# A float32 hybrid decoder trunk: three 256-column products per contraction step become one of 512 and one of 256, in another column order and at other addresses

## Chip, cores and metric

One core of one Trainium2 chip. The metric is the device time of one launch in microseconds (us). Before the change the median of three runs is 1567.65 us (1567.45 to 1567.79).

## What is computed

One decoder layer on 256 tokens with 16 learned meta tokens put ahead of them, model width 2048, all in float32. Cut to what matters:

```python
def rmsnorm(x, g):
    return x * lax.rsqrt(jnp.mean(x * x, axis=-1, keepdims=True) + EPS) * g
...
proj = xn @ w_in                  # 2048 -> 13336 columns: q, k, v, gates of both branches
o_fox = forgetting_attention(fq, fk, fv, ff, b_forget)      # 8 heads of 128
o_gla = gated_linear_attention(gq, gk, gv, g_log)           # 4 heads, chunks of 64
y = sigmoid(gate_fox) * (o_fox @ w_o_fox) + sigmoid(gate_gla) * (o_gla @ w_o_gla)
h = h + y @ w_out
h = h + square(relu(rmsnorm(h) @ w_ff1)) @ w_ff2            # 2048 -> 8192 -> 2048
return rmsnorm(h)[:, N_META:]
```

## The kernel before, in words

Activations are held transposed: channels on the 128 partitions, tokens along the row. A **row tile** is 128 output channels for all tokens; its contraction over 2048 channels runs in 16 steps of 128, here called **k-steps**. Float32 precision is had by splitting: each operand is a high part (rounded to the fp32r format) and a low part (the remainder), and a k-step is three fp32r products that accumulate in one PSUM bank: high weights by high activations, high weights by low activations, low weights by high activations (lines 153, 154 and 155, in `gemm`). Each product has its own load of 128x128 weights into the array. A **token tile** has 256 columns. A **meta tile**, for keys and values, has 272 (the 256 tokens and then the 16 meta tokens).

`stream()` is the order of the row tiles: linear attention (GLA) per head, forgetting attention (FoX) per head, then per output tile two pairs of gates, half a tile each of `of` (FoX outputs) and a tile of `og` (GLA outputs), then 16 tiles on `y` (the output projection), then four rounds of 16 tiles on `x2` (ff1) and 16 on `a` (ff2). Seven tiles of the first stage run side by side while the input arrives (lines 345, 346 and 348). For each tile SyncE loads two halves of the weights (512 KB each), ScalarE rounds them to the high part (`whi`, line 133) and VectorE subtracts for the low part (`wlo`, line 134). Five buffers of each are used in turn, so a half is prepared when TensorE is done with the half five before it. The schedule of each engine is made when the program is built, from this order.

Row tiles alternate between three PSUM banks (pool `pg`). A finished tile is read out of its bank by VectorE in one operation: into `evt` with the norm's factor for gates (lines 464 and 811), into the residual `h` (line 852, `add_residual`), into `evt` with the maximum and the factor for ff1 (line 871, `relu2`), then squared (line 873) and split again into `a` (lines 168 and 169). `in_order` (lines 164 and 165) puts a meta tile's 16 columns back ahead of the tokens in two operations.

Addresses are chosen already: `operand` lays `y`, `of`, `og`, `x2` and `a` out with the high and low parts of 128 tokens in turn, `at` words from the start of the buffer, and `kick` puts the last k-step of `y` and `of` 32 words further (class `Rows`).

Of the kernel before, what the change touches and what calls it, by code (L numbers as in the profile page):

```python
# [7 lines left out]
F32 = mybir.dt.float32  # L8
# [29 lines left out]


class Rows:  # L40

    def __init__(self, most, last):
        self.most, self.last, self.n = most, last, most.shape[1]
        self.shape = [most.shape[0], self.n + 1, *most.shape[2:]]

    def __getitem__(self, at):
        p, k, *rest = at
        if k < self.n:
            return self.most[(p, k, *rest)]
        return self.last[(p, 0, *rest)]  # L50
# [28 lines left out]
def trunk(ctx: ExitStack, tc: tile.TileContext, hT, w_small, w_all, consts, w_alpha2, out):  # L79
# [68 lines left out]
    def gemm(w, x, k0=0, nk=KT, pool=None):  # L148

        ps = bank(pool or pg, "ps")[:, 0 : x.shape[3] if len(x.shape) == 4 else NT]  # L150
        for k in range(nk):
            hi, lo = w(k0 + k)
            nc.tensor.matmul(ps, hi, x[:, k, 0], start=(k == 0), stop=False)  # L153
            nc.tensor.matmul(ps, hi, x[:, k, 1], start=False, stop=False)  # L154
            nc.tensor.matmul(ps, lo, x[:, k, 0], start=False, stop=(k == nk - 1))  # L155
        issued()
        return ps

    def eviction():
        return tmp.tile([P, NT], F32, tag="evt", name=nm("evt"), bufs=2)  # L160

    def in_order(dst, ps, r):

        nc.vector.tensor_tensor(dst[:, NM:NA], ps[:, 0:NT], r[:, NM:NA], op=ALU.mult)
        nc.vector.tensor_tensor(dst[:, 0:NM], ps[:, NT:NA], r[:, 0:NM], op=ALU.mult)
# [45 lines left out]
    def operand(pool, name, nk=KT, at=0, kick=0, **kw):  # L211

        t = pool.tile([P, at + nk * 2 * NT + kick], F32R, name=nm(name), **kw)

        def rows(k, n, at):
            return t[:, at + k * 2 * NT : at + (k + n) * 2 * NT].rearrange("p (k a o t) -> p k o a t", a=2, o=2, t=P)

        return Rows(rows(0, nk - 1, at), rows(nk - 1, 1, at + kick)) if kick else rows(0, nk, at)

    def pair(ap):  # L220
        return ap.rearrange("p (a t) -> p a t", t=P)
# [4 lines left out]
    ROW = 5 * P  # L226
    x_row = keep.tile([P, 64 + KT * ROW], F32R, tag="s1", name="x")[:, 64:]
    xa = x_row.rearrange("p (k o t) -> p k o t", o=2, t=ROW // 2)[:, :, :, 0:NA]
    x_hi, x_lo, x = xa[:, :, 0, :], xa[:, :, 1, :], xa[:, :, :, 0:NT]

    cons = const.tile([P, 425], F32, name="cons")
# [3 lines left out]
    room = keep.tile([P, KT * 2 * NT], F32, tag="s2", name="room")  # L235
# [28 lines left out]
    def first_weights(c0, n, k0):  # L264
        raw = wp.tile([P, HK * P], F32, tag="raw", name=nm("raw"), bufs=RAW)
        hi = wp.tile([P, HK, P], F32R, tag="whi", name=nm("whi"))
        lo = wp.tile([P, HK, P], F32R, tag="wlo", name=nm("wlo"))
# [18 lines left out]
    def square(q):  # L286
        sq = acc if q == 0 else sqs[q % 2]
        nc.scalar.activation(sq, h[:, 4 * q : 4 * q + 4, 0:NA], AF.Square)
        if q:
            nc.vector.tensor_tensor(acc, acc, sq, op=ALU.add)  # L290

# [21 lines left out]
    for s in range(KT // 2):  # L313
# [5 lines left out]
        for kk in range(2):  # L319
            k = 2 * s + kk  # L320
            nc.scalar.activation(x_hi[:, k, 0:NT], h[:, k, NM:NA], AF.Identity, scale=gain(0, k))
            nc.vector.scalar_tensor_tensor(x_lo[:, k, 0:NT], h[:, k, NM:NA], gain(0, k),
                                           x_hi[:, k, 0:NT].bitcast(F32), op0=ALU.mult, op1=ALU.subtract)
            xm = meta[:, k, :]
            nc.gpsimd.tensor_tensor(xm, h[:, k, 0:NM], gain(0, k).to_broadcast([P, NM]), op=ALU.mult)
            nc.gpsimd.tensor_copy(x_hi[:, k, NT:NA], xm)
            nc.gpsimd.tensor_tensor(x_lo[:, k, NT:NA], xm, x_hi[:, k, NT:NA].bitcast(F32), op=ALU.subtract)
# [11 lines left out]
        def products(c, k, part):  # L339
            hi, lo = at[c][0][:, k % 2, :], at[c][1][:, k % 2, :]  # L340
            ps, st, sp = first_ps[c], k == 0, k == KT - 1
            xs = (x if c < NF - 1 else xa)[:, k]
            ps = ps[:, 0 : xs.shape[2]]
            if part == 0:
                nc.tensor.matmul(ps, hi, xs[:, 0], start=st, stop=False)  # L345
                nc.tensor.matmul(ps, hi, xs[:, 1], start=False, stop=False)  # L346
            else:
                nc.tensor.matmul(ps, lo, xs[:, 0], start=False, stop=sp)  # L348
# [110 lines left out]
    def gla_gates(ts):  # L459
        sg = att.tile([P, 4, NT], F32, tag="sg", name=nm("sg"))  # L460
        for i in range(4):
            src = gemm(next_weights(), x) if ts is None else ts[:, i, :]
            t = eviction()
            nc.vector.tensor_tensor(t, src, rbt, op=ALU.mult)
# [26 lines left out]
    def gla_head(hd, sg, ready=None):  # L491
# [11 lines left out]
        def keys(i, ps):  # L503
# [3 lines left out]
            for g, q, n, c in ((0, 0, NM, NT), (0, NM, C - NM, 0), (0, 2 * C, C, C - NM), (1, 0, C, 2 * C - NM),  # L507
                               (1, 2 * C, C, 3 * C - NM)):
                p = (c + NM) % NA
                nc.vector.tensor_tensor(kx[:, i, g, q : q + n], ps[:, c : c + n], en[:, i, p : p + n], op=ALU.mult)  # L510
            nc.vector.tensor_tensor(kz[:, i], *(ap.unsqueeze(1).to_broadcast([P, 4, NB])
                                                for ap in (ps[:, NT - NB : NT], en[:, i, 4 * C :])), op=ALU.mult)

        if ready:
            ps = gemm(next_weights(), xa)
            keys(0, ready[1])
            keys(1, ps)
        else:
            for i in range(2):
                keys(i, gemm(next_weights(), xa))  # L520
        for i in range(2):
            t = ready[0][:, i, :] if ready else gemm(next_weights(), x)
# [62 lines left out]
        for i in range(4):  # L585
            ps = gemm(next_weights(), xa)
            vT = tmp.tile([P, NA], F32, tag="vT", name=nm("vT"))
            in_order(vT, ps, rb)
# [463 lines left out]
```

## Time and profile before

| what | value |
|---|---|
| median of three runs | 1567.65 us |
| the profiled execution | 1567.48 us; its span 1565.8 us, so 1.7 us lie around the span |
| granted TensorE clock, mean | 0.998 |
| TensorE busy with products / with weight loads | 1556.1 / 1553.6 us, 13460 of each |
| VectorE / ScalarE / GpSimd busy | 990.9 / 730.3 / 110.0 us |
| read from memory | 289.32 MB, 187 GB/s on the mean |

How to read it: "PE" rows are products, "PEld" rows are weight loads, and the two run beside each other. A product's recorded duration includes the way through the array, so 276 ns of one does not mean that the next starts 276 ns later; the pace is read from start to start, or from a stretch of time divided by the products in it. "DVE" is VectorE, "ACT" ScalarE, "POOL" GpSimd. An "x770" in a stretch counts products that touch it.

### The profile page before, as it was taken

The numbers are of one execution on the slowest core, as the hardware profiler recorded it, in microseconds if no ns is written. First come the engines' busy times: TensorE is split into PE (matmuls) and PEld (weight loads), VectorE is DVE, ScalarE is ACT, GpSimd is POOL, SyncE is SP. The second block draws the span as 40 slices with busy tenths as digits, with TensorE's granted clock in tenths as the row PEclk, the third lists the DMA queues.
The fourth block names the chain that finished last, engine by engine and source line by source line (L and its number), as shares of the span: only waits on it lengthen the run. The fifth ranks groups of instructions, "written<-read, shape, count | busy, mean of one in ns | idle before, by whom it ended". The sixth has DMA issues, their size and how long they took to land.

```text
span 1565.8 us, 32259 instructions
## 1 busy us (share of the span) xinstructions
PE 1556.1 (99%) x13460; PEld 1553.6 (99%) x13460; DVE 990.9 (63%) x1485; ACT 730.3 (47%) x1006; POOL 110.0 (7%) x197
## 2 busy tenths in 40 slices
PE   9999999999999999999999999999999999999997
PEld 9999999999999999999999999999999999999997
DVE  7897757576665555555666765556655665566655
ACT  6665343444444444444555443344433444344553
POOL 7012000021100000000011000000000000000022
PEclk9999999999999999999999999999999999999999
DMA  9544545555555655656555556566565565665552
GB/s 327 175 150 157 185 157 181 164 194 169 165 162 179 197 190 196 195 191 194 195 192 195 192 191 198 191 196 194 192 197 193 195 195 192 197 192 193 196 183 103
DMA packets 86626, 293.53 MB, mean 187 GB/s; under 512 B 9112, under 2 KB 16800, under 8 KB 86352
## 3 DMA queue, kind: packets, MB, share of 16 engines
q1 hardware_dynamic: 85872, 289.62, 56.8%
q8 instruction: 106, 1.74, 0.4%
q0 software_dynamic: 176, 1.12, 0.2%
q10 hardware_dynamic: 432, 0.72, 0.1%
q14 instruction: 40, 0.33, 0.1%
HBM read 289.32 MB, written 2.11 MB: 186 GB/s over the span
## 4 chain that ended last, share of the span: by engine, by line
PE 99%; POOL 0%; issue 0%; DVE 0%; POOLq 0%; ACT 0%; ACTq 0%
PE ps L154 31%; PE ps L153 31%; PE ps L155 31%; PE ps L345 1%; PE ps L346 1%; PE ps L348 1%; PE ps L921 1%; PE pa L547 1%; PE ps L905 0%; PE po L610 0%; PE warm L308 0%; POOL o L969 0%; PE po L181 0%; PE psa L652 0%; PE pq L726 0%
## 5 line engine op out<-in xcount | busy, mean ns | idle before, releaser
L133 ACT CAST whi<-raw 128x1024 fp32r<-128x1024 f32 x522 | 549.3, 1053 | 752.1 <-PE ps L154 681.5
L134 DVE TENSOR_TENSOR wlo<-raw,whi 128x1024 fp32r<-128x1024 f32 x522 | 639.6, 1226 | 398.0 <-ACT whi L133 388.0
L153 PE MATMUL ps<-x,whi 128*128 128x256 f32 (+1 forms) x2576 | 723.0, 281 | 0.0
L154 PE MATMUL ps<-x,whi 128*128 128x256 f32 (+1 forms) x2576 | 719.6, 279 | 0.0
L155 PE MATMUL ps<-x,wlo 128*128 128x256 f32 (+1 forms) x2576 | 719.5, 279 | 0.0
L155 PEld LDWEIGHTS ps<-x,wlo 128*128 128x128 f32 x2576 | 484.8, 188 | 0.0
L154 PEld LDWEIGHTS ps<-x,whi 128*128 128x128 f32 x2576 | 484.5, 188 | 0.0
L153 PEld LDWEIGHTS ps<-x,whi 128*128 128x128 f32 x2576 | 484.3, 188 | 0.0
L153 PE MATMUL ps<-a,whi 128*128 128x256 f32 x960 | 265.0, 276 | 0.0
L154 PE MATMUL ps<-a,whi 128*128 128x256 f32 x960 | 265.0, 276 | 0.0
L155 PE MATMUL ps<-a,wlo 128*128 128x256 f32 x960 | 265.0, 276 | 0.0
L153 PEld LDWEIGHTS ps<-a,whi 128*128 128x128 f32 x960 | 180.2, 188 | 0.0
L154 PEld LDWEIGHTS ps<-a,whi 128*128 128x128 f32 x960 | 180.2, 188 | 0.0
L155 PEld LDWEIGHTS ps<-a,wlo 128*128 128x128 f32 x960 | 180.2, 188 | 0.0
L849 POOL TENSOR_TENSOR acc<-acc,hsq 128x256 f32<-128x256 f32 x26 | 29.1, 1118 | 747.1 <-ACT hsq L848 747.1
L154 PE MATMUL ps<-y,whi 128*128 128x256 f32 x256 | 70.8, 276 | 0.0
L153 PE MATMUL ps<-y,whi 128*128 128x256 f32 x256 | 70.7, 276 | 0.0
L155 PE MATMUL ps<-y,wlo 128*128 128x256 f32 x256 | 70.7, 276 | 0.0
L154 PE MATMUL ps<-og,whi 128*128 128x256 f32 x256 | 70.7, 276 | 0.0
L153 PE MATMUL ps<-og,whi 128*128 128x256 f32 x256 | 70.7, 276 | 0.0
L155 PE MATMUL ps<-og,wlo 128*128 128x256 f32 x256 | 70.7, 276 | 0.0
L852 DVE TENSOR_TENSOR h<-ps,h 128x256 f32<-128x256 f32 x76 | 32.3, 425 | 39.6 <-PE ps L155 39.6
(296 smaller groups left out, 1455.1 us busy)
## 6 DMA issues: line engine op xcount, KB each, us to landing
raw<-w_all_dram SPq DMA_DIRECT2D x537, 512.0 KB, 4.0
raw<-w_all_dram SPq DMA_DIRECT2D x8, 384.0 KB, 6.6
h<-hT_dram SPq DMA_DIRECT2D x8, 275.0 KB, 6.9
negc<-fdram POOLq DMA_DIRECT2D x1, 1088.0 KB, 7.6
out_dram<-o SPq DMA_DIRECT2D x2, 512.0 KB, 2.6
raw<-w_all_dram SPq DMA_DIRECT2D x2, 256.0 KB, 3.6
room<-w_small_dram SPq DMA_DIRECT2D x1, 320.0 KB, 7.5
out_dram<-o ACTq DMA_DIRECT2D x1, 320.0 KB, 3.1
```

What stands on the lines that cost most here:

```text
L133: nc.scalar.copy(hi[:, k, :], r)
L134: nc.vector.tensor_tensor(lo[:, k, :], r, hi[:, k, :].bitcast(F32), op=ALU.subtract)
L153: nc.tensor.matmul(ps, hi, x[:, k, 0], start=(k == 0), stop=False)
L154: nc.tensor.matmul(ps, hi, x[:, k, 1], start=False, stop=False)
L155: nc.tensor.matmul(ps, lo, x[:, k, 0], start=False, stop=(k == nk - 1))
L345: nc.tensor.matmul(ps, hi, xs[:, 0], start=st, stop=False)
L346: nc.tensor.matmul(ps, hi, xs[:, 1], start=False, stop=False)
L348: nc.tensor.matmul(ps, lo, xs[:, 0], start=False, stop=sp)
L547: nc.tensor.matmul(dst, k[:, a], q[:, a, :], start=(a == 0), stop=(a == 1))
L849: nc.gpsimd.tensor_tensor(acc, acc, sq, op=ALU.add)
L852: nc.vector.tensor_tensor(ht[:, j, :], ps, ht[:, j, :], op=ALU.add)
L921: nc.tensor.matmul(ps[:, NT:], w(k)[0], a[:, k, :, t0 // P], start=(k == 0), stop=(k == KT - 1))
```

## The change

1. **Token tiles.** A k-step is now two products (`mac2`, lines 143 and 144). The high weights take the high and low parts of the activations side by side, 512 columns, into a whole bank; the low weights take the 256 high columns, into its first half. The bank's two halves are added when the tile is read out (`total`): ScalarE copies the second half to SBUF, VectorE adds it to the first. For the residual, `add_residual` has a copy and two additions.
2. **Meta tiles** keep three products of 272 (`mac3`, lines 148, 150 and 152). The row of x is now meta, tokens (high), tokens (low), meta (low), so the low product lands 16 columns further, and `join` adds its 16 meta columns back (a ScalarE copy and a VectorE addition of 16 columns). Columns come out in their own order: `in_order` goes, and `keys` has two operations in place of six.
3. **Order of the columns.** Every such product reads its activations and writes its bank through `steps`: four words, then the four that lie 16 words on, and so on through the row, in four passes.
4. **Addresses.** A 16-word tile `gap` between the pools moves every `wlo` by 64 bytes; x, `y`, `of` and `a` start at other offsets (`a` at 0, 4, 48 and 0 words in the four rounds); `kick` and `Rows` go.
5. **Small ones.** The gates' multiplication goes from VectorE to GpSimd; the corners of a FoX group are split in one pair of operations in place of four; six of the first seven tiles are read by a copy and an addition in place of a copy.

The core of the diff:

```diff
-    def gemm(w, x, k0=0, nk=KT, pool=None):
-        ps = bank(pool or pg, "ps")[:, 0 : x.shape[3] if len(x.shape) == 4 else NT]
+    def steps(ap):
+        return ap.rearrange("p (i a e) -> p a i e", a=4, e=4)
+    def mac2(ps, hi, lo, x, first, last):
+        nc.tensor.matmul(steps(ps), hi, steps(row(x)), start=first, stop=False)
+        nc.tensor.matmul(steps(ps[:, 0:NT]), lo, steps(x[:, 0, :]), start=False, stop=last)
+    def mac3(ps, hi, lo, k, first, last):
+        if hi is not None:
+            nc.tensor.matmul(steps(ps[:, X_LO]), hi, steps(x_lo[:, k]), start=first, stop=False, skip_group_check=True)
+        if lo is not None:
+            nc.tensor.matmul(steps(ps[:, 0:NA]), lo, steps(x_hi[:, k]), start=False, stop=last and hi is None, skip_group_check=True)
+        if hi is not None:
+            nc.tensor.matmul(steps(ps[:, 0:NA]), hi, steps(x_hi[:, k]), start=False, stop=last, skip_group_check=True)
+    def gemm2(w, x, k0=0, nk=KT, pool=None):
+        ps = bank(pool or pg, "ps")
         for k in range(nk):
             hi, lo = w(k0 + k)
-            nc.tensor.matmul(ps, hi, x[:, k, 0], start=(k == 0), stop=False)
-            nc.tensor.matmul(ps, hi, x[:, k, 1], start=False, stop=False)
-            nc.tensor.matmul(ps, lo, x[:, k, 0], start=False, stop=(k == nk - 1))
+            mac2(ps, hi, lo, x[:, k], k == 0, k == nk - 1)
...
+    def join(ps):
+        b = tmp.tile([P, NM], F32, tag="join", name=nm("join"))
+        nc.scalar.copy(b, ps[:, NA : NA + NM])
+        nc.vector.tensor_tensor(ps[:, 0:NM], ps[:, 0:NM], b, op=ALU.add)
+    def total(ps, t=None):
+        b = tmp.tile([P, NT], F32, tag="evb", name=nm("evb"))
+        nc.scalar.copy(b, ps[:, NT:512])
...
+        nc.vector.tensor_tensor(t, ps[:, 0:NT], b, op=ALU.add)
+        return t
...
     def relu2(a, f, ps):
-        t = eviction()
-        nc.vector.scalar_tensor_tensor(t, ps, 0.0, r2b, op0=ALU.max, op1=ALU.mult)
+        t = total(ps)
+        nc.vector.scalar_tensor_tensor(t, t, 0.0, r2b, op0=ALU.max, op1=ALU.mult)
```

TensorE's queue in FoX, where a meta tile ends and a token tile begins. Before (the two rows between are transposes of a finished tile):

```order
L153 MATMUL ps_4271<-x,whi_4266 128x272
L154 MATMUL ps_4271<-x,whi_4266 128x272
L155 MATMUL ps_4271<-x,wlo_4267 128x272
L759 MATMUL pv_4320<-cons,vT_4247 128x128
L760 MATMUL pv_4320<-cons,vT_4247 128x128
L153 MATMUL ps_4342<-x,whi_4331 128x256
L154 MATMUL ps_4342<-x,whi_4331 128x256
L155 MATMUL ps_4342<-x,wlo_4332 128x256
```

Now, at the end of a meta tile of GLA and the start of the token tile behind it; the last numbers are the counts of the column order, four passes of 17, 32 or 16 runs of four:

```order
L148 MATMUL psa_2967<-x,whi_2962 128x4x17x4
L150 MATMUL psa_2967<-x,wlo_2963 128x4x17x4
L152 MATMUL psa_2967<-x,whi_2962 128x4x17x4
L143 MATMUL ps_3033<-x,whi_3022 128x4x32x4
L144 MATMUL ps_3033<-x,wlo_3023 128x4x16x4
```

A meta tile's k-step has three products as it had, in the order high, low, high weights; a token tile's has two, each a single instruction. In the whole program the products fall from 13372 to 9724.

VectorE's queue in ff1, from one reading out of a bank to the next, before:

```order
L871 SCALAR_TENSOR_TENSOR evt_13497<-ps_13448,r2b 128x256
L873 TENSOR_TENSOR asq_13499<-evt_13497 128x256
L134 TENSOR_TENSOR wlo_13639<-raw_13637,whi_13638 128x1024
L169 TENSOR_TENSOR a_12899<-asq_13499,a_12899 128x2x128
L134 TENSOR_TENSOR wlo_13645<-raw_13643,whi_13644 128x1024
```

and now:

```order
L184 TENSOR_TENSOR evt_11633<-ps_11598,evb_11631 128x256
L892 SCALAR_TENSOR_TENSOR evt_11633<-evt_11633,r2b 128x256
L894 TENSOR_TENSOR asq_11636<-evt_11633 128x256
L121 TENSOR_TENSOR wlo_11756<-raw_11754,whi_11755 128x1024
L189 TENSOR_TENSOR a_11207<-asq_11636,a_11207 128x256
L121 TENSOR_TENSOR wlo_11804<-raw_11802,whi_11803 128x1024
```

One operation of 256 columns is added ahead of the others. It waits for ScalarE's copy `evb`, which stands between two weight roundings in ScalarE's queue:

```order
L120 CAST whi_11749<-raw_11748 128x1024
L181 COPY evb_11631<-ps_11598 128x256
L120 CAST whi_11755<-raw_11754 128x1024
L188 CAST a_11207<-asq_11636 128x256
L120 CAST whi_11803<-raw_11802 128x1024
```

The copy is the new row; the rounding of `a` stood between the weight roundings before too. The loads and their order are the same 564 in SyncE's queue.

More of the change, by code (lines that the diff above doesn't have):

```diff
@@ L290, in square, with gap @@
             nc.vector.tensor_tensor(acc, acc, sq, op=ALU.add)
+    def gap():
+        if "gap" not in stages:
+            stages["gap"] = wp.tile([P, 16], F32, tag="gap", name="gap", bufs=1)
     stages = {}
@@ L341, in products @@
             ps, st, sp = first_ps[c], k == 0, k == KT - 1
[L342 to L346, printed above, removed]
+            if c == NF - 1:
+                mac3(ps, hi if part == 0 else None, lo if part else None, k, st, sp and part == 1)
+            elif part == 0:
+                nc.tensor.matmul(steps(ps), hi, steps(row(x[:, k])), start=st, stop=False)
             else:
[L348 removed]
+                nc.tensor.matmul(steps(ps[:, 0:NT]), lo, steps(x[:, k, 0]), start=False, stop=sp)
         if s < KT // 2 - 1:
```

163 lines of the change are left out of this document (81 added, 82 removed).

## The prediction

> **What bounds the kernel now.** I read the page's totals and chain first, then TensorE's waits, then stretches of TensorE's time by stage, then single products and loads.
>
> ```profile
> span 1565.8 us, 32259 instructions
> PE 1556.1 (99%) x13460; PEld 1553.6 (99%) x13460; DVE 990.9 (63%) x1485; ACT 730.3 (47%) x1006; POOL 110.0 (7%) x197
> PE 99%; POOL 0%; issue 0%; DVE 0%; POOLq 0%; ACT 0%; ACTq 0%
> PE warm L308 <- DVE ones L188: 1.3, 1, 1.3
> PE pn L945 <- ACT sq L926: 0.7, 1, 0.7
> ```
>
> TensorE is the bound from end to end: 99% of the chain is its own, and it waits twice, for 2.0 us together. Time can only come from a shorter product pace. The stretches give it (start, end and length in us, products that touch it, granted clock, DMA share, GB/s):
>
> ```profile
> 946.30:1033.34 87.04, 87.04 (x770) 1.00 0.60 194
> 172.70:184.01 11.31, 11.31 (x98) 1.00 0.62 206
> 49.28:67.04 17.76, 17.76 (x147) 1.00 0.60 196
> 0.00:49.28 49.28, 47.97 (x379) 1.00 0.87 287
> ```
>
> The first is a round of ff2, 16 tiles of 16 k-steps: 87.04 / 256 = 0.3400 us per k-step, 113.3 ns per product of 256 columns. The second is two token tiles of GLA: 11.31 / 32 = 353.4 ns, 117.8 per product, for the same instructions at the same clock. So at least 4.5 ns of a product are not columns: they depend on how the streams fall together. The third is three meta tiles: 17.76 / 48 = 370.0 ns, 123.3 per product of 272. The fourth, the first seven tiles, runs with the DMA engines 87% busy.
>
> Is a product paced by its columns or by its weights? The weight loads (mean ns last before the idle time):
>
> ```profile
> L153 PEld LDWEIGHTS ps<-a,whi 128*128 128x128 f32 x960 | 180.2, 188 | 0.0
> L547 PEld LDWEIGHTS pa<-qx,kx 128*128 128x128 f32 x32 | 4.9, 190 | 0.1
> L547 PEld LDWEIGHTS pa<-qx,kx 128*64 128x64 f32 x32 | 2.2, 137 | 0.7
> ```
>
> A load of 128 columns lasts 53 ns longer than one of 64, so 128 stream in about 106 ns. That is 94% of the 113.3 ns: loads and columns go side by side, both without a gap, and 7.3 ns of each product are hand-over or collision.
>
> **The change, part by part.** The count comes from the groups kept apart by shape:
>
> ```profile
> L153 PE MATMUL ps<-x,whi 128*128 128x256 f32 x1952 | 542.1, 278 | 0.0
> L154 PE MATMUL ps<-x,whi 128*128 128x256 f32 x1952 | 540.5, 277 | 0.0
> L155 PE MATMUL ps<-x,wlo 128*128 128x256 f32 x1952 | 540.4, 277 | 0.0
> L153 PE MATMUL ps<-a,whi 128*128 128x256 f32 x960 | 265.0, 276 | 0.0
> L153 PE MATMUL ps<-x,whi 128*128 128x272 f32 x624 | 180.9, 290 | 0.0
> L153 PE MATMUL ps<-y,whi 128*128 128x256 f32 x256 | 70.7, 276 | 0.0
> L153 PE MATMUL ps<-og,whi 128*128 128x256 f32 x256 | 70.7, 276 | 0.0
> L153 PE MATMUL ps<-of,whi 128*128 128x256 f32 x128 | 35.4, 278 | 0.0
> ```
>
> Token k-steps: 1952 + 960 + 256 + 256 + 128 = 3552. (A further 96 in the first stage and 640 of 272.)
>
> *The pair of 512 and 256.* No 512-column product stands in the trace, so it is bounded. While a 512 runs, the load for the 256 behind it has twice its time and is done early; while the 256 runs, the next load again has only that long, so I leave the 256 at 113.3. Low end: the 512 streams at the load's pace with nothing added, 2 x 106 = 212, and the k-step is 212 + 113.3 = 325.3. High end, from the nearest product whose columns outlast its load, the 272: 123.3 less 106 x 272/256 = 112.6 leaves 10.7, so 212 + 10.7 + 113.3 = 336.0. If columns cost what they cost now, 768 x 113.3/256 = 340.0, and nothing is gained; if every product falls into the slow pace, 353.4. I take **328.5**, a third of the way up between the first two: in a 272 the load streams through 94% of the product, in a 512 through half, so less of the 10.7 should be met. Saved per k-step 11.5 ns, x 3552 = **-40.8 us** (ends -52.2 and -14.2; with the others 0 and +47.6).
>
> The Trainium skill, "TensorE: Matmul & The Clock Gate", section "Back-to-back issue gap", gives N/2.4 + 2.5 ns for a warm product alone, an estimate of 215.8 + 109.2 = 325.0 per k-step here and 53 us saved. Its 109.2 for 256 columns is 4.1 below the 113.3 measured, so the measurement decides for the 256.
>
> *The slow pace.* The token group of x and x2 lasts 542.1 us where 1952 of `a`'s 276 ns would be 538.8; with its two sisters (540.5 and 540.4) the excess is at most 6.6 us, and part of it lies at changes to other work. New addresses may end it or spread it: **-2 us** (0 to -6.6).
>
> *Meta tiles.* 640 k-steps keep three products and three loads. Columns and addresses change, the count doesn't: **0**, between -15 (three of 112.6 + 3 in place of 370) and +9 (13.4 each, the step between the two paces).
>
> *First stage.* Its 96 token k-steps could give 96 x 11.5 = 1.1 us, but the row above has DMA near its limit there: **0**.
>
> *Reading out.* Each of the 3552 / 16 = 222 token tiles gains a ScalarE copy and a VectorE addition:
>
> ```profile
> L134 DVE TENSOR_TENSOR wlo<-raw,whi 128x1024 fp32r<-128x1024 f32 x522 | 639.6, 1226 | 398.0 <-ACT whi L133 388.0
> L852 DVE TENSOR_TENSOR h<-ps,h 128x256 f32<-128x256 f32 x76 | 32.3, 425 | 39.6 <-PE ps L155 39.6
> L133 ACT CAST whi<-raw 128x1024 fp32r<-128x1024 f32 x522 | 549.3, 1053 | 752.1 <-PE ps L154 681.5 <-issue 60.9 <-ACT hsq L848 1.9
> L168 ACT CAST a<-asq 128x256 fp32r<-128x256 f32 x64 | 25.9, 406 | 0.1
> 80.00:90.00 10.00, 10.00 (x86) 9.62 (x84) 10.00 (x31) 5.12 (x9) 1.35 (x2) 1.00 0.32 106
> ```
>
> The program has 174 more VectorE additions and 265 more ScalarE copies, small ones among them; at 425 and 406 ns that is at most 74 and 108 us, or 70% and 55% of a span of 1524. TensorE's products hide it: ScalarE's idle 752 us ahead of the roundings is for TensorE (681.5) to give up buffers, so preparation runs ahead. The narrow place is GLA's first heads, where VectorE is busy for all 10 us of a stretch (third pair in the row); there the tiles are mostly meta tiles, whose six or two operations become fewer. If this cover went, each late addition would show with its 0.43 us.
>
> *Hand-overs between stages.* An ff1 round's last tile feeds ff2's 16th k-step:
>
> ```profile
> 1120.51 1.05 ACT L133 CAST whi<-raw 128x1024 fp32r<-128x1024 f32 x1 [1.67 <-PE ps L154]
> 1120.58 0.43 DVE L871 SCALAR_TENSOR_TENSOR evt<-ps,r2b 128x256 f32<-128x256 f32 x1 [0.48 <-PE ps L155]
> 1121.50 0.41 ACT L168 CAST a<-asq 128x256 fp32r<-128x256 f32 x1
> 1122.74 0.42 DVE L169 TENSOR_TENSOR a<-asq,a 128x256 fp32r<-128x256 f32 x1
> ```
>
> ff2 began at 1120.38 and wants the last `a` 15 k-steps later, at 1125.5; it is ready at 1123.16, 2.3 us early. Now the copy stands behind the rounding that starts as the tile ends: 1120.51 + 1.05 + 0.41 + 0.43 = 1122.40 for the maximum that began at 1120.58, so 1.8 us later, or 3.0 if a `wlo` of 1.23 slips between. The wanted time comes 15 x 11.5 ns = 0.2 us sooner, so 2.1 us of slack are left: 0 to 0.9 us of waiting at each of four such places and one ahead of x2: **+1 us** (0 to +4).
>
> *Sum*, on the profiled execution: 1565.8 - 40.8 - 2 + 0 + 0 + 1 = 1524.0, and 1.7 around the span: **1525.7 us**, against 1567.48 for that execution, which is 0.2 below the median.
>
> **The rivals.**
>
> *More is gained.* If the steps keep reads of weights and of columns apart, the k-step goes to 325.3 and the meta tiles lose 15: 1565.8 - 52.2 - 2 - 15 + 1 + 1.7 = **1499**. For it: 4.5 ns per product already come and go with the pace alone. Against: nothing of the steps' effect is in the trace.
>
> *Less is gained.* Columns, not loads, pace the product. For it: 113.3/256 and 123.3/272 are 0.443 and 0.453 ns per column, nearly one rate. At 336.0: **1552**; at 340.0, with the slow pace gone, **1566**, no change. Against: 117.8 for the same 256 columns. That the change isn't carried out is ruled out by the queues: each 512 is one instruction.
>
> *Slower: the runs of four collide more.* Every product jumps 16 words after each four, on the way in and in the bank. If that throws each load and column stream into the slow pace, a k-step is 353.4: +47.6, less some 4 already paid: 1565.8 + 43.6 + 1 + 1.7 = **1612**. It decides from a 512 product of over 226.7 ns beside a 256 of 113.3. For it: the paces of 113.3 and 117.8 show that the way two streams fall together matters, and one of them now changes place every four words. Against: each run is read and written whole, four words on end.
>
> The Trainium skill, "Advanced Engine Details and Errata", section "PSUM Cachelines", says that a bank's pattern with gaps slows products significantly, and in the next line that two neighbours on end are what best throughput needs. By its first line this rival comes; by its second, runs of four are free. No product of the trace writes with gaps, so no run here shows which.
>
> **How the numbers follow.** Forecast, k-step 325 to 333: 1511 to 1541, chance 0.50. More gained, 1488 to 1511: 0.14. Less, 1541 to 1564: 0.13. Within 0.2% (3.1 us, about what a measurement of this kernel can tell from no change): 0.05. Slower, around 1612: 0.18. So faster 0.77, same 0.05, slower 0.18. The range goes from the more-gained case's end through no change with its width, 1488 to 1572, and leaves out the slower rival.
>
> **What would show it.** ff2's rounds: 84.1 us for 256 k-steps in place of 87.04. Starts 215 ns apart behind a 512 and 113 behind a 256 confirm the hand-over; 227 and 113 say that columns pace; 109 behind a 256 says that the load wasn't the limit. Meta tiles away from 370 ns per k-step say that order and addresses act by themselves. VectorE or ScalarE as what TensorE waits for, by more than the 2.0 us of before, would make the reading-out wrong. A k-step over 340 makes the whole forecast wrong.

## The result, and the profile after

The changed kernel takes **1567.36 us** (median of 12 runs, 1566.89 to 1567.79), the kernel before 1567.84 us on the same chip (12 runs, 1567.45 to 1568.13): a ratio of 0.9997, 95% interval 0.9988 to 1.0006. The change makes no difference that can be measured. The profiled execution took 1566.89 us, its span 1565.1.

The page of the changed kernel:

```profile
span 1565.1 us, 25427 instructions
PE 1553.5 (99%) x9812; PEld 1408.5 (90%) x9812; DVE 1060.0 (68%) x1659; ACT 790.4 (50%) x1271; POOL 128.2 (8%) x213
PE 97%; ACT 1%; DVE 1%; issue 0%; DMA 0%; POOL 0%; SPq 0%; POOLq 0%; ACTq 0%; DVEq 0%
```

A quarter of the products and of the weight loads is gone (13460 to 9812), and TensorE is still the bound from end to end. So the products that are left take longer, all in all by as much as was removed. What TensorE waited for:

```profile
PE warm L328 <- DVE ones L208: 1.3, 1, 1.3
PE ps L143 <- DVE x L879: 0.7, 1, 0.7
PE ps L364 <- ACT whi L293: 0.7, 2, 0.4
PE pn L966 <- ACT sq L947: 0.7, 1, 0.7
PE pa L562 <- DVE kx L524: 0.5, 1, 0.5
```

3.9 us in place of 2.0, and none of it behind a bank that is read out. By the letter of the prediction's sign (waits for VectorE or ScalarE of more than 2.0 us) the reading out would be wrong; but what is waited for here are operands (`ones`, `x`, `whi`, `kx`, `sq`), not `evb` or `evt`. Two operations of the reading out, and ScalarE's rounding, in the groups by line (busy time, mean ns of one, idle time before them):

```profile
L184 DVE TENSOR_TENSOR evt<-ps,evb 128x256 f32<-128x256 f32 x158 | 65.7, 417 | 0.5 <-ACT evb L181 0.5
L181 ACT COPY evb<-ps 128x256 f32<-128x256 f32 x160 | 58.3, 365 | 1.3 <-DVE evt L184 0.9 <-PE ps L366 0.3
L120 ACT CAST whi<-raw 128x1024 fp32r<-128x1024 f32 x522 | 548.2, 1050 | 633.0 <-PE ps L143 474.6 <-issue 113.5 <-PE psa L152 40.4
```

ScalarE still idles 633 us ahead of the roundings, most of it for TensorE. The reading out is hidden; the answer is in the pace. Stretches of the changed kernel (start, end and length in us, products that touch it): ff2's first, second and third round, two token tiles of GLA, and two meta tiles:

```profile
943.80:1031.14 87.34, 87.34 (x514) 77.39 (x513) 52.04 (x66) 38.19 (x49) 0.00 (x0) 1.00 0.57 194
1118.53:1206.40 87.87, 87.87 (x515) 77.90 (x514) 52.05 (x66) 38.23 (x49) 0.00 (x0) 1.00 0.56 192
1293.44:1380.09 86.65, 86.65 (x515) 77.37 (x513) 52.04 (x67) 38.20 (x49) 0.00 (x0) 1.00 0.57 195
172.46:183.43 10.97, 10.97 (x66) 9.73 (x65) 9.35 (x20) 5.77 (x10) 0.00 (x0) 1.00 0.56 191
234.74:246.55 11.81, 11.81 (x99) 11.81 (x97) 11.38 (x26) 4.86 (x7) 0.00 (x0) 1.00 0.53 179
```

Divided by 256, the rounds give 341.2, 343.2 and 338.5 ns per k-step, where the three products of before took 340.0. The rounds run the same instructions on the same loads; the place of `a` differs (0, 4 and 48 words from the buffer's start, that is 64, 80 and 0 modulo 256 bytes: the remainder of the address by 256, which is what "at 64" means from here on). ff1's rounds on x2, which keeps its place, lie between 340.0 and 341.7 by their starts. These two token tiles of GLA are at 10.97 / 32 = 342.8 (before 353.4). They are among the best of the attention's: most other token tiles there take 5.57 us for 16 k-steps, 348 ns each, where they took 5.74 or 5.54 before (359 or 346). The meta tiles shown are at 11.81 / 32 = 369.1 (before 370.0). Three products in a row of TensorE in ff2's second round:

```profile
1149.74 0.39 PE L143 MATMUL ps<-a,whi 128*128 128x512 f32 x1
1149.97 0.28 PE L144 MATMUL ps<-a,wlo 128*128 128x256 f32 x1
1150.09 0.39 PE L143 MATMUL ps<-a,whi 128*128 128x512 f32 x1
```

0.23 us behind the 512 and 0.12 behind the 256. Over all pairs on x2 the starts lie 226.7 and 114.4 ns apart: the sign that the prediction gave for "columns pace".

Stage by stage, from the starts of the first product on `of`, `y` and x2 (488.15, 771.65 and 859.0 us before; 482.50, 767.26 and 855.16 now) and the span's end: attention gains 5.65 us, the mixing loses 1.3, the output projection 0.55, ff1 and ff2 3.1.

### The profile page after: what moved, and what is told of

It reads as the page before. It is cut to its first block, busy times and chain, and to the rows that moved or that the text cites. A ratio compares the mean times of both kernels' runs of the same rounds, so it can differ in the third digit from the quotient of the medians.

```text
span 1565.1 us, 25427 instructions
## 1 busy us (share of the span) xinstructions
PE 1553.5 (99%) x9812; PEld 1408.5 (90%) x9812; DVE 1060.0 (68%) x1659; ACT 790.4 (50%) x1271; POOL 128.2 (8%) x213
## 4 chain that ended last, share of the span: by engine, by line
PE 97%; ACT 1%; DVE 1%; issue 0%; DMA 0%; POOL 0%; SPq 0%; POOLq 0%; ACTq 0%; DVEq 0%
PE ps L143 51%; PE ps L144 26%; PE psa L152 4%; PE psa L148 4%; PE psa L150 4%; PE ps L364 1%; PE ps L366 1%; PE ps L942 1%; PE pa L562 1%; PE ps L926 0%; ACT whi L120 0%; DVE wlo L121 0%; DMA raw<-w_all_dram 0%; PE po L625 0%; POOL o L990 0%
## 5 line engine op out<-in xcount | busy, mean ns | idle before, releaser
L143 PE MATMUL ps<-x,whi 128*128 128x512 f32 x1952 | 671.7, 389 | 0.7 <-DVE x L879 0.7
L144 PE MATMUL ps<-x,wlo 128*128 128x256 f32 x1952 | 540.0, 277 | 0.0
L143 PEld LDWEIGHTS ps<-x,whi 128*128 128x128 f32 x1952 | 366.2, 188 | 75.5 <-DVE x L879 1.1
L144 PEld LDWEIGHTS ps<-x,wlo 128*128 128x128 f32 x1952 | 367.3, 188 | 0.1
L143 PE MATMUL ps<-a,whi 128*128 128x512 f32 x960 | 327.3, 387 | 0.0
L143 PEld LDWEIGHTS ps<-a,whi 128*128 128x128 f32 x960 | 179.6, 187 | 36.4
L148 PE MATMUL psa<-x,whi 128*128 128x272 f32 x640 | 182.3, 286 | 0.0
L152 PE MATMUL psa<-x,whi 128*128 128x272 f32 x640 | 180.6, 283 | 0.0
L150 PE MATMUL psa<-x,wlo 128*128 128x272 f32 x624 | 176.9, 283 | 0.0
L148 PEld LDWEIGHTS psa<-x,whi 128*128 128x128 f32 x640 | 120.4, 188 | 0.3
L152 PEld LDWEIGHTS psa<-x,whi 128*128 128x128 f32 x640 | 120.2, 188 | 0.0
L150 PEld LDWEIGHTS psa<-x,wlo 128*128 128x128 f32 x624 | 117.1, 188 | 0.0
```

The source lines that it names most:

```text
L143: nc.tensor.matmul(steps(ps), hi, steps(row(x)), start=first, stop=False)
L144: nc.tensor.matmul(steps(ps[:, 0:NT]), lo, steps(x[:, 0, :]), start=False, stop=last)
L148: nc.tensor.matmul(steps(ps[:, X_LO]), hi, steps(x_lo[:, k]), start=first, stop=False, skip_group_check=True)
L150: nc.tensor.matmul(steps(ps[:, 0:NA]), lo, steps(x_hi[:, k]), start=False, stop=last and hi is None, skip_group_check=True)
L152: nc.tensor.matmul(steps(ps[:, 0:NA]), hi, steps(x_hi[:, k]), start=False, stop=last, skip_group_check=True)
```

## Experiments

The runs undo or vary one part at a time; the kernel before took 1567.5 to 1567.9 us beside all of them. "The changed kernel" is 1567.4. Ratios are to the kernel before, with their 95% interval; "..." in a diff marks lines left out.

**The order of four, undone** (contig):

```diff
-        return ap.rearrange("p (i a e) -> p a i e", a=4, e=4)
+        return ap
```

> The changed kernel with every product's columns read and written on end, without the order of four words and then four that lie 16 on; pairs of 512 and 256, addresses and reading out as they are. Columns theory (an fp32r column costs 0.443 ns whatever its product and its load are): starts 226 to 228 ns apart behind a 512 and 113 to 116 behind a 256 stay, the time stays within some 5 us of 1567; a step to the slow pace of before (117.8 per 256) is possible in some tiles and would show as 235.5 and 117.8. Rival, the order of four eats the gain of the pair: k-steps fall to 325 to 333 ns and the time to 1525 to 1545 us. Rival, the order of four is what keeps the slow pace and collisions away: k-steps go towards 353 and the time to 1590 or more.

Measured: 1605.6 us, ratio 1.0241 (1.0227 to 1.0254). On x2 the starts are 231.6 and 120.3 ns apart, 351.9 per k-step. The last theory is the one that holds: columns on end cost the kernel 38 us, 8 of them in the meta tiles (their products start 127.0 ns apart in place of 122.8), so the runs of four do not eat a gain of the pair. The columns theory (227 and 113 whatever the order) falls.

**Half the weights** (half_w): 64 output channels in place of 128 in 14 of 16 k-steps of ff1 and ff2; the other 64 are left out there.

```diff
-            mac2(ps, hi, lo, x[:, k], k == 0, k == nk - 1)
+            m = 64 if ff[0] and 0 < k < nk - 1 else P
+            mac2(ps[0:m], hi[:, 0:m], lo[:, 0:m], x[:, k], k == 0, k == nk - 1)
...
```

> The changed kernel with weights of 64 output channels in place of 128 in 14 of the 16 k-steps of the 124 tiles of ff1 and ff2 (1736 k-steps; the other 64 output channels are left out there). A load then streams for about 53 ns instead of 106. Columns theory: 226.7 and 113.3 stay, k-step 340, time 1565 to 1568. Load theory (what a product takes beyond its cycles comes from the load that streams beside it, by pace or by collision): the 256 falls to 109 or below, the 512 to 220 or below, k-step 320 to 330, time 1537 to 1552.

Measured: 1560.1 us (0.9952, 0.9933 to 0.9970). Both theories miss. ff1's second and ff2's second round:

```profile
1028.96:1114.82 85.86, 85.86 (x514) 64.53 (x513) 62.77 (x94) 42.54 (x63) 0.00 (x0) 1.00 0.60 196
1114.82:1202.57 87.75, 87.75 (x514) 66.26 (x513) 52.11 (x67) 38.24 (x49) 0.00 (x0) 1.00 0.60 192
```

335.4 ns per k-step where the activations lie at 64 (341.4 in the changed kernel), 342.8 where they lie at 80 (343.2). The stream of the load beside the columns matters, by some 6 ns in one place and by none in the other.

**Half the columns in the low product** (low128; in 15 of 16 k-steps of ff1 and ff2 the low weights meet only the first 128 tokens):

```diff
-            mac2(ps, hi, lo, x[:, k], k == 0, k == nk - 1)
+            n = P if ff[0] and k else NT
+            nc.tensor.matmul(steps(ps), hi, steps(row(x[:, k])), start=k == 0, stop=False)
+            nc.tensor.matmul(steps(ps[:, 0:n]), lo, steps(x[:, k, 0, 0:n]), start=False, stop=k == nk - 1)
...
```

> The changed kernel with 128 columns in place of 256 in the product of the low weights in 15 of the 16 k-steps of the 124 tiles of ff1 and ff2 (1860 k-steps; low weights by the second 128 tokens are left out there). Columns theory alone: 56.7 ns behind such a product, k-step 283, time 1462. If a load of 106 ns is a floor that a product can't go below: 106 to 113 behind it, k-step 333 to 340, time 1554 to 1567; between them if a load may start during the 512 before.

Measured: 1559.5 us (0.9947, 0.9929 to 0.9966). TensorE's loads in this kernel, and its products:

```profile
1149.99 0.19 PEld L162 LDWEIGHTS ps<-a,whi 128*128 128x128 f32 x1
1150.10 0.19 PEld L163 LDWEIGHTS ps<-a,wlo 128*128 128x128 f32 x1
1150.32 0.19 PEld L162 LDWEIGHTS ps<-a,whi 128*128 128x128 f32 x1
```

```profile
1149.71 0.43 PE L162 MATMUL ps<-a,whi 128*128 128x512 f32 x1
1149.98 0.22 PE L163 MATMUL ps<-a,wlo 128*128 128x128 f32 x1
1150.04 0.43 PE L162 MATMUL ps<-a,whi 128*128 128x512 f32 x1
```

The product of 128 lets the next start after 0.06 us (1149.98 to 1150.04), but a 512 now has 0.27 behind it (1149.71 to 1149.98) in place of 0.23: its load begins with the 128 ahead of it, and the next load 0.11 later, so a 512 that follows a 128 stands for its weights. On x2, where a 128 lies on both sides of the 512, the two take 279.0 and 57.7 ns, 336.7 together, which is 226.7 + 110.0; in ff1's second round the load for a 128 starts 108.6 ns behind the load ahead of it. So a load of 128 columns acts as a floor of some 109 ns under each product, near the 106 that I had read from 190 and 137 ns; with 256 columns it doesn't bind.

**The pair, undone** (triple): the 512 is two products of 256, all else as changed.

```diff
-        nc.tensor.matmul(steps(ps), hi, steps(row(x)), start=first, stop=False)
-        nc.tensor.matmul(steps(ps[:, 0:NT]), lo, steps(x[:, 0, :]), start=False, stop=last)
+        nc.tensor.matmul(steps(ps[:, 0:NT]), hi, steps(x[:, 0, :]), start=first, stop=False, skip_group_check=True)
+        nc.tensor.matmul(steps(ps[:, NT:]), hi, steps(x[:, 1, :]), start=False, stop=last, skip_group_check=True)
+        nc.tensor.matmul(steps(ps[:, 0:NT]), lo, steps(x[:, 0, :]), start=False, stop=last, skip_group_check=True)
```

> The changed kernel with the pair undone alone: the 512 is two products of 256 again, each with its own load of the same weights, in the order of four, at the places and with the reading out of the changed kernel. Columns theory (768 columns cost the same in two products as in three): k-step 340 to 345, time 1564 to 1575. Rival, the pair saves a hand-over of some 3 ns or more per product that the order of four had cost: each product 115 to 118, k-step 345 to 354, time 1578 to 1608. Rival, the pair itself costs what the order of four gains: three of 109 to 112, k-step under 336, time under 1550.

Measured: 1567.05 us (0.9996, 0.9987 to 1.0005), 340.5 ns per k-step in ff2's first round. The number is as the columns theory has it: at the changed kernel's places the pair is worth nothing.

**Two-byte operands** (bf16): weights and activations of ff1 and ff2 in bf16 parts.

```diff
+        if half:
+            hi, lo = (t.bitcast(BF16)[:, :, 0:P] for t in (hi, lo))
...
-    x2 = operand(keep, "x2", at=0, tag="s2")
+    x2 = operand(keep, "x2", at=0, half=True, tag="s2")
```

> The changed kernel with weights and activations of ff1 and ff2 (124 tiles and the last four) in bf16 high and low parts in place of fp32r ones, so that a column and a weight are 2 bytes in place of 4 (the parts hold fewer bits; the computation is rougher there). Theory, what a column costs beyond a cycle comes from reading 4-byte activations and 4-byte weights side by side: 512 and 256 go towards 216 and 109, k-step 325, which is 17 ns less in 1984 k-steps, time about 1533. Rival, the pace is the array's or the bank's and not that of the reading: 226.7 and 113.3 stay, time 1565 to 1568.

Measured: 1571.9 us (1.0026, 1.0016 to 1.0036). In ff2's second round the starts are 228.6 and 114.8 ns apart, 343.4 per k-step as with four bytes (343.2). Where the fp32r rounds were faster, bf16 is not: 344.0 in ff2's first round and 343.3 in its third, against 341.2 and 338.5. So in this order half the bytes gain nothing. But at the end, where the same kernel runs 256 columns without the order of four (two runs of 128 on end):

```profile
1559.52 1.15 PE L949 MATMUL ps<-a,whi_last 128*128 128x256 bf16 x9
1560.50 0.28 PE L973 MATMUL pn<-acc,ones 128*128 128x128 f32 x1
```

nine products fill 0.98 us, 109 ns each; the 256s in fours just ahead of these tiles (line 933) start 114.6 ns apart. So there the order of four costs a bf16 product some 5 ns per 256. In the changed kernel the same two groups in fp32r go at medians of 115 in fours and 113 on end: it is the fp32r pair for which the order gains, not the single 256.

**No gap** (nogap): without the 16-word tile, `wlo` lies at 128 modulo 256 bytes as `whi` does, instead of at 192.

```diff
         hi = wp.tile([P, HK, P], F32R, tag="whi", name=nm("whi"))
-        gap()
         lo = wp.tile([P, HK, P], F32R, tag="wlo", name=nm("wlo"))
```

> The changed kernel without the 16-word tile between the weights' buffers: every wlo lies at 128 modulo 256 bytes as whi does, where the change has 192 (of, too, moves, from 64 to 0). Theory, only how the activations' stream and the weights' stream stand to each other counts: k-steps change in both directions by up to 7 ns, and the time goes away from 1567 by 3 us or more. Rival, the weights' place has no part: 1565 to 1568.

Measured: **1549.4 us** (0.9882, 0.9868 to 0.9895). 64 bytes cost the changed kernel 18.0 us (with the gap `of` moves too, from 0 to 64; its 128 k-steps go from 337.5 to 341.3 ns, 0.5 us of it). ff2's first three rounds:

```profile
934.67:1020.87 86.20, 86.20 (x514) 76.53 (x513) 52.05 (x67) 38.22 (x49) 0.00 (x0) 1.00 0.61 196
1107.06:1192.57 85.51, 85.51 (x515) 77.12 (x513) 52.05 (x67) 38.23 (x49) 0.00 (x0) 1.00 0.61 198
1278.78:1364.14 85.36, 85.36 (x514) 76.76 (x513) 52.03 (x67) 38.23 (x49) 0.00 (x0) 1.00 0.60 198
```

336.7, 334.0 and 333.4 ns in place of 341.2, 343.2 and 338.5. In the second round the starts are 220.5 and 113.5 apart: fewer ns for the same columns, so it wasn't the columns alone that paced the changed kernel. The meta tiles lose (their products 124.6 in place of 122.8 ns, 3.5 us in all).

**No gap and no pair** (triple_nogap; nogap with the diff of triple):

> The kernel nogap with the pair undone: three products of 256, in the order of four, wlo at 128 modulo 256 bytes as whi. In nogap a 512 took 220.5 and a 256 113.5 on y, 7.2 and 6.8 ns beyond their cycles. Theory, a product costs some 7 ns beyond its cycles whatever its length, once nothing else disturbs it (my pair, with a smaller saving): three products of 111.7 to 113.5, k-step 337 to 340.5, time 1555 to 1573. Rival, columns alone (768 columns cost the same in two products as in three, as with the gap): k-step 334 to 337, time 1548 to 1552.

Measured: 1577.6 us (1.0062, 1.0047 to 1.0077). ff2's first and second round:

```profile
949.71:1037.61 87.90, 87.90 (x771) 87.90 (x769) 51.95 (x66) 38.16 (x49) 0.00 (x0) 1.00 0.61 193
1125.50:1213.57 88.07, 88.07 (x771) 88.07 (x769) 51.92 (x66) 38.09 (x49) 0.00 (x0) 1.00 0.60 190
```

343.4 and 344.0 ns: slower than either theory had it for three products, so the pair is worth 6.7 and 10.0 ns per k-step here, **28.2 us** in all. Without the gap the pair saves about what the prediction said. And the gap is no loss by itself: with three products the kernel is 10.5 us faster with it (triple, 1567.05) than without (1577.6). Pair and gap can't be priced apart.

**No gap, columns on end** (contig_nogap; nogap with the diff of contig):

> The kernel nogap with every product's columns on end: the pair, without the order of four and without the gap. Theory, the order of four keeps the two streams out of each other's way and is needed with or without the gap: k-steps of 347 to 354 as in contig, time 1590 to 1606. Rival, the gap is what hurt, and a pair on end is as good as one in fours: k-step 334 to 337, time 1548 to 1555. Between: near the 340 of the kernel before, 1565 to 1570.

Measured: 1610.7 us (1.0276, 1.0260 to 1.0291):

```profile
967.13:1057.57 90.44, 90.44 (x514) 78.51 (x513) 52.05 (x66) 38.22 (x49) 0.00 (x0) 1.00 0.58 187
1148.02:1237.64 89.62, 89.62 (x514) 78.31 (x513) 52.04 (x66) 38.17 (x49) 0.00 (x0) 1.00 0.59 188
```

353.3 and 350.1 ns. With the pair, the order of four is worth 38 us with the gap and 61 us without it.

**All three undone** (plain has the diffs of triple, contig and nogap; plain64 the activations at 64 modulo 256 bytes besides, as before):

```diff
-    x_row = keep.tile([P, 52 + KT * ROW + 12], F32R, tag="s1", name="x")[:, 52 : 52 + KT * ROW].rearrange(
+    x_row = keep.tile([P, 48 + KT * ROW + 16], F32R, tag="s1", name="x")[:, 48 : 48 + KT * ROW].rearrange(
...
-    y = operand(keep, "y", at=4, tag="s1")
+    y = operand(keep, "y", at=0, tag="s1")
...
-        a = operand(keep, "a", at=(0, 4, 48, 0)[g], tag="s1")
+        a = operand(keep, "a", at=0, tag="s1")
```

> The changed kernel with the pair, the order of four and the gap all undone; reading out by copy and addition, the layout of x, the other places and the meta tiles' arrangement stay. If what is left costs nothing (reading out hidden), columns on end in products of 256 go at 113.3 to 117.8 as before: 1565 to 1580 by how many tiles fall into the slow pace. If the reading out costs something of its own, idle time of TensorE ahead of products would show it, by more than the 4 us of the changed kernel.

Measured: 1603.2 us (1597.5 to 1609.9 in four executions; 1.0228, 1.0189 to 1.0267), with no more waiting of TensorE than in the changed kernel: the reading out isn't it.

> The kernel plain (three products of 256 on end, no gap) with x's tokens, y, of, og, x2 and a all at 64 modulo 256 bytes, as in the kernel before. Theory, plain's 35 us over the kernel before are the change's new places (118.7 to 119.5 ns a product at 80 and 0, 113.4 at 64): x and y and the second and third a fall from 119 to 113.3, time 1567 to 1575. Rival, the reading out or the meta tiles' row is what costs: 1590 or more.

Measured: 1598.6, 1599.2 and 1598.8 us in three executions and 1577.3 in a fourth (1.0164, 1.0101 to 1.0227). y, of and og went to 113.3 ns per product as expected, ff1 and ff2 to 117.8; ff2's second round:

```profile
1134.63:1225.08 90.45, 90.45 (x770) 90.45 (x769) 51.96 (x66) 38.17 (x49) 0.00 (x0) 1.00 0.58 186
```

353.3 ns, the slow pace that the kernel before shows in GLA. One program, 21 us apart from one execution to the next. That this program falls into one of two paces and stays there is my reading of it, not shown: the faster execution left no profile. I thought that `kick` (the last k-step 32 words further) was what put the kernel before into the faster one, and took it away:

```diff
-    of = operand(late, "of", FOX_H, at=0, kick=32)
+    of = operand(late, "of", FOX_H, at=0)
...
-    y = operand(keep, "y", at=64, kick=32, tag="s1")
+    y = operand(keep, "y", at=64, tag="s1")
```

> The kernel before without kick: the last k-step of y and of lies where the others do. Theory, streams on end lock into one of two paces, 113.3 or 117.8 ns a product, and stay in it through whole rounds until something shifts them; kick is what shifts the ff rounds to the faster one: without it 124 tiles of 48 products stay 4.4 ns slower, 26 us, 1585 to 1598, or, where an execution happens to lock well, 1568; executions differ by more than 5 us. Rival, kick has no part in it and plain64's 31 us come from something else that the change brings: 1566 to 1570 in all.

Measured: 1566.7 us (0.9994, 0.9985 to 1.0004), ff2 at 113.3 ns as before. That theory falls. What puts plain64's ff rounds into the slow pace (its high x low product goes to the other half of the bank, its activations lie 256 and not 128 to a run, its reading out is another) is open; none was tried alone.

**The places of the activations.** at48 puts y, x2 and the four `a` to 0 modulo 256 bytes in the changed kernel, all0 also x, og and of:

```diff
-    y = operand(keep, "y", at=4, tag="s1")
+    y = operand(keep, "y", at=48, tag="s1")
...
-    x2 = operand(keep, "x2", at=0, tag="s2")
+    x2 = operand(keep, "x2", at=48, tag="s2")
...
-        a = operand(keep, "a", at=(0, 4, 48, 0)[g], tag="s1")
+        a = operand(keep, "a", at=48, tag="s1")
```

> The changed kernel with y, x2 and all four a at 48 words from the start of their buffers (0 modulo 256 bytes), where the changed kernel has 4, 0 and 0, 4, 48, 0. Places theory (the start of an operand is worth up to 5 ns of a k-step: 338.3 ns was read at 48, 341.4 at 0, 343.4 at 4): all ff1 and ff2 rounds and y go to 338.3, which is 256 x 5.1 for y, 256 x (3.1 + 5.1 + 3.1) for a and some 1024 x 2.2 for x2, 6 us in all: 1561. Rival, the place has no part in it and the differences come from which buffers and times meet: no change, 1566 to 1568.

In all0 x starts at 32 words in place of 52, og at 48 in place of 0, of at 0 in place of 16:

> The kernel at48 with x, og and of as well at 0 modulo 256 bytes (x from 80, og and of from 64; the meta tiles' operands go from 16 and 80 to 192 and 0). Places theory: x's token tiles go from 229.5 + 115.8 to 224.6 + 113.9, 6.8 ns in 1024 k-steps, og and of by 2.7 in 384, 8 us in all, meta tiles unknown: 1553, between 1549 and 1557. Rival, the place of the ff rounds alone did it: 1561.

Measured: 1561.3 us (0.9961, 0.9947 to 0.9974) and 1556.1 (0.9925, 0.9912 to 0.9939), both as the places theory has them. ff2's second round in at48, 338.4 ns at the place where the changed kernel's third has 338.5:

```profile
1115.18:1201.80 86.62, 86.62 (x514) 77.38 (x513) 52.04 (x67) 38.17 (x49) 0.00 (x0) 1.00 0.60 196
```

**The place of the weights.** Is it the distance between the two loads, or the place 192? both192 has the gap ahead of `whi`, so that both are at 192; gap32 has 32 words, `wlo` at 0 (the one diff, then the other):

```diff
+        gap()
         hi = wp.tile([P, HK, P], F32R, tag="whi", name=nm("whi"))
-        gap()
...
-        stages["gap"] = wp.tile([P, 16], F32, tag="gap", name="gap", bufs=1)
+        stages["gap"] = wp.tile([P, 32], F32, tag="gap", name="gap", bufs=1)
```

> The changed kernel with the 16-word tile ahead of whi's buffers in place of ahead of wlo's: whi and wlo both lie at 192 modulo 256 bytes (the change has 128 and 192, nogap has 128 and 128). Theory, what costs the 18 us is that the two loads that follow each other start at different places: as in nogap, k-steps of 334 to 337, time 1547 to 1553. Rival, a load at 192 costs it against these activations, whichever load it is: 1567 or, with two such loads, more, up to 1585.

> The changed kernel with 32 words in place of 16 between the weights' buffers: wlo at 0 modulo 256 bytes, 128 bytes from whi's place in place of 64 (of moves from 64 to 128). Theory, different places of the two loads cost the time, whatever the distance: 1562 to 1572. Rival, only the place 192 does: near nogap, 1547 to 1555.

Measured: 1559.1 us (0.9945, 0.9931 to 0.9960) and 1571.8 (1.0028, 1.0017 to 1.0040). The kernels with equal places are faster than those with unequal ones (1549.4 and 1559.1 against 1567.4 and 1571.8), but 192 for both costs 10 us too, so neither theory is enough. The rounds of gap32 (ff2's second at 80, ff1's second at 64) show that it depends on the activations' place as well:

```profile
1123.24:1212.52 89.28, 89.28 (x514) 78.23 (x513) 52.12 (x67) 38.20 (x49) 0.00 (x0) 1.00 0.57 189
1037.05:1123.24 86.19, 86.19 (x514) 77.00 (x513) 62.75 (x94) 42.53 (x63) 0.00 (x0) 1.00 0.60 195
```

348.8 ns at 80, but 336.7 at 64, no worse than with no gap at all. Nor do the places fix the pace by themselves. ff1's second and third round in both192 read the same x2 at the same places, with the same instructions:

```profile
1028.69:1116.30 87.61, 87.61 (x514) 77.42 (x513) 62.80 (x94) 42.48 (x63) 0.00 (x0) 1.00 0.60 193
1203.38:1288.75 85.37, 85.37 (x515) 76.81 (x513) 62.74 (x94) 42.80 (x63) 0.00 (x0) 1.00 0.60 197
```

342.2 and 333.5 ns, so at these places the pair too has a slow and a fast pace, and such slow rounds are part of the 10 us. The runs show that moving a buffer changes the time; by what rule, and what selects the pace at one place, stays open.

**The version that beats both.** nogap0 is nogap with the diff of at48 and og at 48 words, so y, x2, og and `a` lie at 0 modulo 256 bytes; best has y back at 4 words, at 80:

> The kernel nogap with y, x2, og and a at 0 modulo 256 bytes, the version that the runs so far point to. In nogap the k-steps were 336.7 at 64, 334.0 at 80 and 333.5 at 0. Places theory: 2.9 to 3.3 ns in 1024 k-steps of x2, 448 of a and 256 of og, 5 us: 1543 to 1546. Rival, with wlo beside whi the operands' place no longer counts: 1549.

> The kernel nogap0 with y back at 4 words (80 modulo 256 bytes), where nogap read 220.5 + 113.5 and nogap0, with y at 0, 226.8 + 114.8; the version that should beat both kernels. 7.6 ns in 256 k-steps: 1543. Rival, y's pace is not set by its place alone: 1545.

Measured: 1545.1 us (0.9860, 0.9843 to 0.9876) and **1543.0 us** (0.9844, 0.9829 to 0.9858), 24 us under both kernels. In nogap0 `y` took 341.6 ns per k-step where `a`, in the same buffer at the same 48 words, took 333.3; at 80 `y` took 333.7. What makes 0 bad for `y` alone is not known. ff2's first round in best:

```profile
932.46:1017.79 85.33, 85.33 (x514) 76.76 (x513) 52.08 (x67) 38.25 (x49) 0.00 (x0) 1.00 0.60 197
```

333.3 ns, 221.3 behind a 512 and 112.0 behind a 256. And best with the pair undone:

> The version called best with the pair undone: three products of 256 in the order of four, at its places. Theory, the pair is worth what it was worth in nogap (a product of its own costs some 7 ns beyond its cycles, and three in a row disturb each other besides): 1570 to 1575, 27 to 32 us over best. Rival, at better places three products come to 3 x 112 = 336 ns and the pair is worth 10 us or less: 1545 to 1553.

Measured: 1579.5 us (1.0071, 1.0054 to 1.0088):

```profile
950.05:1038.12 88.07, 88.07 (x771) 88.07 (x769) 51.92 (x66) 38.14 (x49) 0.00 (x0) 1.00 0.59 191
```

344.0 against 333.3: the pair is worth 10.7 ns per k-step here, 36.5 us in all (the theory had 27 to 32).

## Why the prediction failed

The time lay within the range, but the forecast was a gain of 42 us and none came. Where it went, in times of whole kernels: from the kernel before to three products in the changed order, places and reading out, without the gap, 1567.8 to 1577.6, **+9.7**; the pair **-28.2**; the gap **+18.0**; sum -0.5, as measured. The shares hold for this order only. Taken the other way, three products with the gap come to 1567.05 (-0.8), and the pair then adds 0.3.

- *What bounds the kernel*: right. TensorE's products are the chain before, after and in every run (95 to 99% of the chain).
- *The pair of 512 and 256* (328.5 per k-step, -40.8 us, ends -52.2 and -14.2): a saving is there, and its size lies within the ends, 28.2 us in nogap and 36.5 in best, 10.7 ns per k-step there against 11.5. The 512 took 221.3 rather than 215, the 256 112.0 rather than 113.3. That it comes from the load streaming beside only half of a 512, as I argued, is not shown: halving the loads (half_w) moved the k-step by 6 ns at one place and by none at another. But the saving was subtracted whatever the places, and it is not there at all of them; in the changed kernel the same pair took 226.7 + 114.4 and was worth nothing (triple). The 340.0 from which I subtracted doesn't hold everywhere either: in the order of four three products take 340.5 with the gap and 343.4 to 344.0 without it.
- *The slow pace* ("New addresses may end it or spread it: -2 us", 0 to -6.6): **the step that failed.** It is where I priced part 4 of the change, its addresses, by the only two paces the trace had and only for the better. In the attention stage the slow pace gave way in part (tiles of GLA 353.4 to 342.8, others 359 to 348, but some 346 to 348); the stage gained 5.65 us, 3.8 of them in the meta tiles. But with the pair the 64 bytes ahead of `wlo` cost 18.0 us. With the gap in place, 64 and 80 in place of 0 for the activations cost 6.1 (at48) to 11.3 us (all0); without it 4.2 (nogap to nogap0). The sum added the pair and the addresses as terms that don't touch each other; the runs show that the addresses decide what the pair is worth. Why they do is open.
- *Meta tiles* (0, -15 to +9): within its ends. On the mean over all, products start 122.8 ns apart in place of 124.8, 3.8 us less; the 370.0 per k-step of the prediction was one stretch, the mean was 374.4.
- *First stage* (0): the first meta tile after it starts at 49.53 in place of 49.28 us.
- *Reading out* (hidden): right, though TensorE's waits rose from 2.0 to 3.9 us. VectorE got 69 us more work and ScalarE 60, and no bank was waited for.
- *Hand-overs* (+1): right. One place, ahead of x2, waits 0.7 us for VectorE; the four from ff1 to ff2 don't.
- *The rivals*: "less is gained" at 340.0 gave 1566, and 227 and 113 ns were its sign. Time and sign came, the reason behind them did not: in nogap the same columns go at 220.5 and 113.5. That it named the right time is luck. "Runs of four collide more" was wrong in sign: on end, the kernel with the pair is 38 to 61 us slower.

The Trainium skill, "Advanced Engine Details and Errata", section "PSUM Cachelines", has patterns with gaps slow products and, one line on, two neighbours on end enough for best throughput. For fp32r neither line tells what came: at the same places a pair in fours takes 334.0 to 336.7 ns per k-step, on end 350.1 to 353.3 (nogap and contig_nogap).

The Trainium skill, "TensorE: Matmul & The Clock Gate", section "Back-to-back issue gap", gives N/2.4 + 2.5 ns for a warm product alone, an estimate of 109.2 for 256 columns and 215.8 for 512. bf16 on end agrees (109 ns); fp32r pairs came to 112.0 and 221.3 in best and to 226.7 for the 512 in the changed kernel, and the measurement decides.

## What to carry to other kernels

When a change merges products or alters how operands are read, the places of weights and activations in memory are a term of their own, as large as the change itself: try the merge at several offsets of both before judging it, with the rest held fixed, and don't add up the gains of parts that were priced one at a time. A ratio that fits "time per column" at one set of places doesn't prove that columns pace; vary the place, not only the length.

## What the hardware showed that I had not expected

- 64 bytes in the place of one of two weight buffers moved a TensorE-bound kernel of 1567 us by 18 us one way with the pair and by 10.5 us the other way with three products. 16 bytes in the place of the activations moved a k-step by 2.0 ns (341.2 at 64, 343.2 at 80; 338.5 at 0). Without the gap the order of the places is another (336.7, 334.0, 333.4). And one place can have two paces in one execution (342.2 and 333.5 on x2 in both192).
- With three products on end the same program (plain64) took 1577.3 us in one execution and 1598.6 to 1599.2 in three; in the profiled one, of the three, every product of ff1 and ff2 keeps a pace of 117.8 ns, while `y` and og keep 113.3. In the order of four single 512s of one round vary from 219 to 235 ns, but executions agree within 0.2%.
- Operands of half the width gained nothing in the order of four (343.3 to 344.0 ns per k-step in ff2), and loads of half the width gained 6 ns or none, by place.
